# Convolution gate projection by seven products, with weight sums made early and kept in DRAM

## The chip, the cores and the metric

The kernel runs on all 8 cores of one Trainium2 chip (two dies, cores 0 to 3 and 4 to 7). Every core works on its own prompt sequence and its share of the sample rows. A time is the device time of the slowest core in microseconds (us), so one slow core sets it. In this case the granted TensorE clock differs between runs, between chips and between the cores of one run. This text often uses a second measure: the **full-clock span**, the mean span of all cores whose mean granted clock was 0.99 or more, over all timed runs of a kernel on one chip.

## The reference, cut to what matters

A trunk of two layers. The even layer has a pooling mixer and a gated recurrence (HGRN, 6 heads). The odd layer is the gated convolution that is changed here. A squared-ReLU MLP of width 4096 follows each of them: MLP X after the even layer, MLP Y after the odd one.

```python
def odd_layer(h, conv_prev, w_in, conv_w, w_out):       # h: 2048 tokens x 1024 per core
    bg, cg, hv = jnp.split(h @ w_in, 3, axis=-1)         # three 1024 x 1024 projections
    z = cg * hv
    ext = jnp.concatenate([conv_prev, z], axis=1)
    conv = conv_w[0] * ext[:, 0:t_]                      # three taps along the tokens
    for j in range(1, CONV_WIDTH):
        conv = conv + conv_w[j] * ext[:, j:j + t_]
    return (bg * conv) @ w_out, ext[:, -CONV_BUF:]
```

## The kernel before

Most projections go by "seven products" (Strassen's scheme in Winograd's form): a 2x2 block product takes 7 block products instead of 8, for some sums of operands. One group of seven (`quad`) takes 28 matmuls of 128x512 where the straight way takes 32. Its partial results are handed from one PSUM bank to another by a copy on ACT. Ahead of a copy into a bank that its last writer did not fill, the kernel runs one extra identity matmul of 128x512 over that bank (`bits`).

```python
def quad(prods, evac, mark=None, hook=None, raw=False):
    def bits(k):
        if not B_ps[k].full:
            yield MMG([(bank(k), identh, <identity x4>, True, True)], ...)   # 1 matmul 128x512
    def copy(k, src):                                    # "bank copy"
        yield from bits(k)
        op = ACT(bank(k), bank(src), AF.Copy, ...)       # PE must wait for it
    ...
    yield from prod(1, a, True); yield from fifth()
    yield from copy(b, a)
    yield from prod(6, b, False); yield from prod(2, a, False)
    yield from copy(d, b)
    yield from prod(7, d, False)
    ... # cut: products 3, 4 and the evacuations
```

In the convolution only cg and hv went by seven products, one unit per 128 channels; the gate B went straight. DVE made the weight sums inside the stage, and the taps ran on 512 tokens at a time:

```python
def conv_wsums(p):                                       # 4 sums a unit, 16 units
    for c in range(8):
        for o, a, b, op in (("s1","a21","a22",add), ("s2","s1","a11",sub), ("a21","a11","a21",sub), ("s4","a12","s2",sub)):
            yield TT(W[o], W[a], W[b], op, ...)          # 128x512 f16
def conv_bg(p, c, kb):                                   # gate: straight, 16 matmuls a unit
    for t in (2 * p, 2 * p + 1):
        yield MMG([(bank(k), W[bg], hT[:, k8, tokslice(t)], k8 == 0, k8 == 7) for k8 in range(8)], ...)
def taps(D, BD, src, Bsrc, i):                           # in conv_unit, twice a unit
    yield ACT(D, src[:, 0:512], AF.Copy, scale=w0)
    yield STT(D, src[:, 1:513], w1, D, mult, add)
    yield STT(D, src[:, 2:514], w2, D, mult, add)
    yield TT(mixT[:, c, tokslice(t)], bank(kb[i]), D, mult)
```

The order of the instructions on each engine is fixed when the program is built. A list scheduler simulates the engines with modelled durations and a modelled delay from one engine to the next (`HOP`), and emits whichever operation can start first.

```python
HOP = 0.06
start = max(self.free[eng], self.ready(op) + HOP)
# ACT, second part of the program ("late"):
occ = 0.14 + n / 1280.0 + (0.19 if accum is not None else 0.0) + (0.0 if in_psum(in_) else 0.03)
# DVE tensor-tensor:
occ = 0.12 + n / (1925.0 if two else 965.0) + (0.05 if not ps and not two and n > 256 else 0.0)
# a PSUM bank: the one free first; one that still needs bits counts as free 1 us later
return t if want is None or bufs[0].full == want else t + 1.0
```

Of the kernel before, what the change touches and what calls it, by code (L numbers as in the profile page):

```python
# [25 lines left out]
U_OO = 33  # L26
NU = 35
# [7 lines left out]
ROWPAGE = 100  # L35
CPAGES = [0, 5, NPG + 3, NPG + 11]
GPAGES = [10, NPG, NPG + 8]
SHPAGE = NPG + 16
CSP = 11
CSTAGE = 8  # L40
ZSTAGE = 9
# [14 lines left out]
NFIRST = 7  # L56
CLASSIC = 1
M_ORDER = [(0, u) for u in range(U_WO, U_FF0 + 4 * CLASSIC)] + [(1, u) for u in (U_WO, U_WO + 1)]
M_ORDER2 = [(1, u) for u in range(U_CONV, NU)] + [(2, u) for u in range(U_CONV, U_OO)]
# [6 lines left out]
OOPRIO = 299  # L66
FINPRIO = 250
POOLX = 15

HOP = 0.06  # L70
PE_MARGIN = 0.30
# [47 lines left out]
class Prog:  # L119
# [29 lines left out]

    def est(self, op):  # L150
        return max(self.free[op.eng], self.ready(op) + HOP + op.margin)
# [49 lines left out]
    def emit(self, op):  # L201
        eng = op.eng
        start = max(self.free[eng], self.ready(op) + HOP)
        if eng == "pe" and self.filler is not None and start < WARM_END:
            at = max(self.free[eng], max(max(b.wt, b.rt) for b in op.W) + HOP)
            n = int((start - at) * WARM_SHARE / self.filler[0])
            if n > 0:
                make = self.filler[1]
                self.filler = None
                self.emit(make(n, op.W))  # L210
                self.filler = (0.22, make)
                start = max(self.free[eng], self.ready(op) + HOP)
# [182 lines left out]
def build():  # L395
# [15 lines left out]
    w2w = din("w2w", [2, NW2, 4, 128, 2048])  # L411
    gcols_d = din("gcols", [128, 40])
# [27 lines left out]
    with ExitStack() as es:  # L440
# [88 lines left out]
        def ACT(out, in_, func, R, W, scale=1.0, bias=0.0, accum=None, t=None):  # L529
# [5 lines left out]
            if late:  # L535
                occ = 0.14 + n / 1280.0 + (0.19 if accum is not None else 0.0) + (0.0 if in_psum(in_) else 0.03)
                if (not isinstance(scale, float) or not isinstance(bias, float)) and n > 8:
                    occ += 0.09
# [7 lines left out]

        def TT(out, in0, in1, op, R, W, eng="dve", fast=False):
            n = fsz(out)
            if late:
                ps = in_psum(in0) or in_psum(in1)  # L550
                two = not ps and all(a.dtype in (F16, BF16) for a in (in0, in1, out))
                occ = 0.12 + n / (1925.0 if two else 965.0) + (0.05 if not ps and not two and n > 256 else 0.0)
# [7 lines left out]
        def TS(out, in0, s1, op0, R, W, s2=None, op1=None):  # L560
# [4 lines left out]
            occ = 0.134 + fsz(out) / 1800.0 if late else 0.07 + fsz(out) / 1920.0  # L565
            return Op("dve", f, R, W, occ, occ + 0.08)

        def STT(out, in0, scalar, in1, op0, op1, R, W):
            occ = 0.184 + fsz(out) / 964.0 if late else 0.1 + fsz(out) / 850.0
            return Op("dve", lambda e: e.scalar_tensor_tensor(out=out, in0=in0, scalar=scalar, in1=in1,  # L570
                                                              op0=op0, op1=op1), R, W, occ, occ + 0.08)

        def CP(out, in_, R, W, eng="dve"):
            occ = (0.12 if late else 0.07) + fsz(out) / (1925.0 if eng == "dve" else 465.0)
            return Op(eng, lambda e: e.tensor_copy(out=out, in_=in_), R, W, occ, occ + 0.08)
# [82 lines left out]
        for c in range(8):  # L658
            unit_cols[U_CONV + c] = 3072
# [5 lines left out]
        hown = set()  # L665

        def loader(order, pool, mine):
            for key in order:
                it = yield Alloc(pool)
                s = it[0]  # L670
                u = key[1]
                ncol = unit_cols[u]
# [114 lines left out]
        junks = Pool(junk_items[:1])  # L787

        def junk_of(page):

            return pgf(page).bitcast(F16) if page < ROWPAGE else mixT[:, page - ROWPAGE, 0:1024]
# [5 lines left out]
        def norm(b, n, done):  # L797
            jp = junks0 if n == 0 else junks
# [86 lines left out]
        def sample_rows(src, Bs, page, dst, ds):  # L885

            stage = pgf(page, 2)[0:16, :]
            for half in range(2):
# [4 lines left out]
                yield CP(stage[:, half * 512:(half + 1) * 512], bank(k)[0:16, :], [B_ps[k]], pgb(page + half))  # L893
                banks.give(k)
            yield DMA("sp", ds, [(dst, stage)], pgb(page, 2), (), 65536)
# [645 lines left out]

        def quad(prods, evac, mark=None, hook=None, raw=False):
# [67 lines left out]
        def wmlp(tag, l, seq, n_in, n_out, smp, gates):  # L1610
# [14 lines left out]
            if early_t:  # L1625
                cb["h"] = (m02, m12, m03)

            def rings():
                for k in range(NSLOT):
# [9 lines left out]
                    if k == 2:  # L1639
                        cb["h"], cb["w"] = ((m02, m12, m03), (m00, m10, rb[4])) if early_t else ((m00, m10, rb[4]), (m02, m12, m03))  # L1640
# [12 lines left out]
            def w2raw(gi):  # L1653
                return [rb[6], rb[7], rb[8], rb[9]] if gi % 2 == 0 else [ex_blk(1), ex_blk(2), rb[8], rb[9]]
# [17 lines left out]
            def load1():  # L1672
                for n in range(4 * NS):
# [4 lines left out]
                    if n == 3:  # L1678
                        yield up(*gates.get("ex", ()))
# [24 lines left out]
            def combh():  # L1704
                for i, p in enumerate(pairs):
# [15 lines left out]
                    yield up(T("rb", 2))  # L1721
# [39 lines left out]
            def ff1_unit(n):  # L1761
                if True:
# [3 lines left out]
                    if n < 2:  # L1766
                        yield up(T("rb", 0), T("rb", 1), T("rb", 2), *gates["hid"])
# [22 lines left out]
                    def evac(what, k, n=n, gi=gi, u=u, k0=k0, c0=c0):  # L1790
# [12 lines left out]
                        if what in ("12", "22"):  # L1803
                            yield up(T("g", n))
                            yield Op("dve", lambda e: e._custom_dve(TENSOR_ADD_SAT, out=v, in0=bank(k), in1=gst(n), s0=3e38, s1=0.0),  # L1805
                                     [B_ps[k], B_gst[n % 2]], B, 0.68, 0.76)
# [71 lines left out]
            def ff2_quad(m):  # L1878
                if True:
# [8 lines left out]
                    for j in (m % 4,):  # L1888
# [18 lines left out]
                        def evac(what, k, j=j, left=left, last=last, t0=t0, p=p):  # L1907
                            for r, h in {"g": ((0, 1), (1, 1)), "11": ((0, 0),), "12": ((0, 1),), "21": ((1, 0),),
                                         "22": ((1, 1),)}[what]:
# [3 lines left out]
                                left[r] -= 1  # L1913
                                if what == "21" and last and n_out == 4 and p == pairs[-1] and j == 3:
                                    flags.add("lastadd")
                                if left[r] == 0 and last:
                                    if p == pairs[-1]:
                                        S.spawn(norm(b, n_out, ("h%d" % n_out, b)), FINPRIO)
# [89 lines left out]
        def oo():  # L2008
# [15 lines left out]
            t1, t2 = oo_t  # L2024
            t4 = Blk(q4(hg[:, :].bitcast(F16)), [B_hg] * 4)
            yield up("zrows")
            for b in B_oot:
                for pb in flat(pgb(8, 4)):
                    inherit(b, pb)
# [8 lines left out]

            def run(i):
                for p, j in todo[i::2]:  # L2040
                    yield from oo_quad(p, j, b11, b21, b12, b22, t1, t2, t4)
# [3 lines left out]
            for k in keys:  # L2045
                drop(k)

        def oo_sums(p):
# [3 lines left out]
            yield up(*[("cproj", c, t) for c in range(8) for t in (t0, t0 + 1)])  # L2052
# [13 lines left out]
        def oo_norm(b):  # L2066
# [3 lines left out]
            elif b >= 4:  # L2070
                yield up("cquads")
            yield from norm(b, 3, ("h3", b))

        def oo_quad(p, j, b11, b21, t3, b22, t1, t2, t4):
# [3 lines left out]
            yield up("oot", *[("cmix", c, t) for c in range(8) for t in (t0, t0 + 1)])  # L2078
# [10 lines left out]
            def evac(what, k):  # L2089
                for r, h in {"g": ((0, 1), (1, 1)), "11": ((0, 0),), "12": ((0, 1),), "21": ((1, 0),), "22": ((1, 1),)}[what]:  # L2090
# [10 lines left out]
        cva = [[Buf(f"cv{q}{n}") for n in "ABGZ"] for q in range(2)]  # L2101
        B_oot = [Buf("oot0"), Buf("oot1")]

        def conv_s4(p, q):
            if q == 0:
                return band[:, :, :].rearrange("p g t -> p (g t)")[:, 0:512], [B_band]
            if p == 0:
                return hg[:, 0:256].bitcast(F16), flat(B_hg)
            return prevT[:, :, :, :].rearrange("p r c t -> p (r c t)").bitcast(F16), [B_prev]
        oo_t = [Blk(q4(arena[:, 4104 + 1024 * i:5128 + 1024 * i].bitcast(F16)), [[B_oot[i]]] * 4) for i in range(2)]  # L2110

        def conv_bufs(q):
            o = 2052 * q
            A, B, G, Z = arena[:, o:o + 512], arena[:, o + 512:o + 1024], arena[:, o + 1024:o + 1538], arena[:, o + 1538:o + 2052]
            return A, B, G, Z, [[b] for b in cva[q]]

        cwts = {}

        def conv_take(p, c):
            s = slot_of[(1 + p, U_CONV + c)]  # L2120
            W = {}
            for i, n in enumerate(("a11", "a12", "a21", "a22", "bg0", "bg1", "s1", "s2")):
                q = Buf(f"cw{n}")
                src = B_ring[s][i // 4]
                q.w, q.wt = src.w, src.wt
                W[n] = (ring[:, s, 512 * i:512 * i + 512], [q])
            W["s4"] = conv_s4(p, c % 2)
            cwts[p, c] = W

        def conv_put(p, c):  # L2130
            key = (1 + p, U_CONV + c)
            s = slot_of[key]
            for i, n in enumerate(("a11", "a12", "a21", "a22", "bg0", "bg1", "s1", "s2")):
                inherit(B_ring[s][i // 4], cwts[p, c][n][1][0])
            used(key, 2 - p)

        def conv_wsums(p):
            for c in range(8):
                yield loaded((1 + p, U_CONV + c))
                conv_take(p, c)  # L2140
                flags.add(("cw", p, c))
                W = cwts[p, c]
                for i, (o, a, b, op) in enumerate((("s1", "a21", "a22", ALU.add), ("s2", "s1", "a11", ALU.subtract),
                                                   ("a21", "a11", "a21", ALU.subtract), ("s4", "a12", "s2", ALU.subtract))):
                    if o == "s4":
                        if p or c > 1:
                            yield up(("cquad", p, c - 2) if c > 1 else ("cquad", 0, 6 + c))
                        if p:
                            yield up("zrows")
                    yield TT(W[o][0], W[a][0], W[b][0], op, W[a][1] + W[b][1], W[o][1], fast=True)  # L2150
                    flags.add(("cs", p, c, i + 1))

        def conv_t(p):
            return [mix_blk(0, 2), mix_blk(1, 2), mix_blk(0, 3), mix_blk(1, 3)] if p == 0 else \
                [ex_blk(0), ex_blk(1), ex_blk(2), hT_blk(1, 1)]

        def conv_hsums(p):
# [5 lines left out]
            for i, o, a, b, op in ((3, t3, b22, b12, ALU.subtract), (2, t2, t3, b11, ALU.add), (1, t1, b22, t2, ALU.subtract),  # L2163
                                   (4, t4, b21, t2, ALU.subtract)):
                if p and i == 4:
                    yield up(*[("cproj", c, 1) for c in range(8)])
# [3 lines left out]
        def conv_bg(p, c, kb):  # L2170
# [384 lines left out]
```

## Time and profile before

| | before |
|---|---|
| timed runs | 1441.06 us median of 3 (1439.7 to 1441.55) |
| profiled run | span 1415.1 to 1420.7 us by core, granted clock 0.993 to 0.995 |
| busy on core 2 | PE 97%, DVE 80%, ACT 63% |

The page of the kernel before starts with the span and the busy time of each engine; part 4 is the chain of work that ended last.

```profile
span 1420.7 us, 25535 instructions; the slowest of 8 cores (1415.1 to 1420.7 us)
...
PE 1377.5 (97%) x9160; PEld 698.0 (49%) x9182; DVE 1133.3 (80%) x2096; ACT 895.0 (63%) x1806; POOL 189.3 (13%) x274
...
PE 88%; DVE 5%; DMA 2%; ACT 2%; issue 1%; SPq 0%; DVEq 0%; POOL 0%; ACTq 0%; POOLq 0%
...
```

PE is busy 97% of the span and is 88% of the chain. At a given clock only fewer matmuls, or fewer pauses of PE, shorten this kernel. Next, busy time in stretches of the span, still of the kernel before. The first column after the colon is the length, then come PE, PEld, DVE, ACT and POOL busy with the number of instructions, then the granted clock (1.00 is full), the DMA share and GB/s. Rows: MLP X, convolution with the transition to Y, MLP Y.

```profile
...
420.00:775.00 355.00, 351.55 (x2153) 168.07 (x2151) 276.01 (x487) 223.91 (x431) 30.11 (x57) 1.00 0.46 77
775.00:980.00 205.00, 196.48 (x1177) 93.18 (x1176) 182.29 (x386) 98.90 (x187) 15.89 (x30) 0.98 0.45 74
980.00:1400.00 420.00, 419.31 (x2450) 197.35 (x2448) 328.87 (x567) 264.81 (x521) 31.70 (x60) 1.00 0.47 88
...
```

Length minus PE busy is PE's idle time: 3.4, 8.5 and 0.7 us. In the middle row the clock is below full. Next are PE's waits over the whole run (what was waited for: total us, times, longest).

```profile
...
PE pp L598 <- DVE hT L558: 3.8, 2, 2.5
PE pp L598 <- ACT pp L532: 3.3, 5, 1.0
PE pp L600 <- DVE x_sb L558: 2.7, 4, 1.2
...
```

"ACT pp" is a bank copy: PE waits until ACT has moved one PSUM bank into another. The timeline of PE at the transition from the convolution to MLP Y shows where the idle time sits (start, length, group; in brackets the idle time before the group and who ended it).

```profile
...
968.44 1.03 PE L600 MATMUL pp<-arena,hT 128*128 128x512 f16 x4
972.00 0.38 PE L598 MATMUL pp<-identh,arena 128*128 128x128 f16 x4 [2.53 <-DVE hT L558]
973.61 0.59 PE L598 MATMUL pp<-identh,arena 128*128 128x128 f16 x4 [1.22 <-DVE hT L558]
975.40 1.86 PE L600 MATMUL pp<-ring,mixT 128*128 128x512 f16 x4 [1.20 <-DVE x_sb L558]
977.06 1.91 PE L598 MATMUL pp<-arena,hT 128*128 128x512 f16 x4
...
981.18 1.03 PE L598 MATMUL pp<-ring,mixT 128*128 128x512 f16 x4
...
```

PE waits 2.53, 1.22 and 1.20 us for DVE. After that, four matmuls last 1.86 us from first start to last end, where later ones last 1.03: the granted clock was 0.50 from 974 to 979 us (the same view of stretches as above). By start times the next three groups of four take 1.66, 1.70 and 1.13 us instead of 0.86, so 1.9 us are lost to the clock. Before the low clock stood waits of 2.53 and 1.22 us with 0.4 us of small matmuls between them; what sets it off is not shown.

### The profile page before, as it was taken

The numbers are of one execution on the slowest core, as the hardware profiler recorded it, in microseconds if no ns is written. First come the engines' busy times: TensorE is split into PE (matmuls) and PEld (weight loads), VectorE is DVE, ScalarE is ACT, GpSimd is POOL, SyncE is SP. The second block draws the span as 40 slices with busy tenths as digits, with TensorE's granted clock in tenths as the row PEclk, the third lists the DMA queues.
The fourth block names the chain that finished last, engine by engine and source line by source line (L and its number), as shares of the span: only waits on it lengthen the run. The fifth ranks groups of instructions, "written<-read, shape, count | busy, mean of one in ns | idle before, by whom it ended". The sixth has DMA issues, their size and how long they took to land.

```text
span 1420.7 us, 25535 instructions; the slowest of 8 cores (1415.1 to 1420.7 us)
## 1 busy us (share of the span) xinstructions
PE 1377.5 (97%) x9160; PEld 698.0 (49%) x9182; DVE 1133.3 (80%) x2096; ACT 895.0 (63%) x1806; POOL 189.3 (13%) x274
## 2 busy tenths in 40 slices
PE   8989999999999999999999999998999999999996
PEld 3666555654444444454445444444444544444442
DVE  5887898886677778877769999979778788977767
ACT  5868888874455656864667434455647757755655
POOL 1121134333200110010000010000100100100100
PEclk9999999999999999999999999999999999999998
DMA  8681353397644743642633644440735626644612
GB/s 187 158 134 32 89 137 92 93 203 145 153 90 74 120 73 57 109 78 46 116 53 56 101 79 72 67 83 1 126 62 96 105 43 107 163 107 74 119 31 119
DMA packets 64281, 136.68 MB, mean 96 GB/s; under 512 B 6751, under 2 KB 33598, under 8 KB 64142
## 3 DMA queue, kind: packets, MB, share of 16 engines
q0 software_dynamic: 28256, 97.07, 41.0%
q1 hardware_dynamic: 35902, 37.97, 8.7%
q8 instruction: 77, 1.26, 0.4%
q14 instruction: 46, 0.38, 0.1%
HBM read 216.61 MB, written 15.54 MB: 163 GB/s over the span
## 4 chain that ended last, share of the span: by engine, by line
PE 88%; DVE 5%; DMA 2%; ACT 2%; issue 1%; SPq 0%; DVEq 0%; POOL 0%; ACTq 0%; POOLq 0%
PE pp L598 44%; PE pp L600 43%; DMA ring<-wst 1%; PE pp L610 1%; ACT arena L532 1%; DMA x_sb<-xp 1%; DVE hT L558 1%; DVE x_sb L558 1%; DVE arena L558 1%; DVE arena L570 1%; DVE mixT L558 0%; DVE gsm L558 0%; DVE x_sb L570 0%; ACT pp L532 0%; DVE mixT L563 0%
## 5 line engine op out<-in xcount | busy, mean ns | idle before, releaser
L532 ACT ACTIVATE pp<-pp 128x512 f32<-128x512 f32 x432 | 246.4, 581 | 298.8 <-PE pp L598 204.3
L558 DVE TENSOR_TENSOR x_sb<-x_sb,pp 128x512 f32<-128x512 f32 x496 | 322.1, 682 | 92.5 <-PE pp L598 37.0
L600 PE MATMUL pp<-hT,ring 128*128 128x512 f16 (+1 forms) x1700 | 301.0, 318 | 3.8 <-ACT arena L532 1.0
L600 PEld LDWEIGHTS pp<-hT,ring 128*128 128x128 f16 x1700 | 131.6, 97 | 138.0 <-issue 6.2
L532 ACT ACTIVATE arena<-arena 128x512 f16<-128x512 f16 (+1 forms) x287 | 174.2, 623 | 13.2 <-DVE arena L1805 6.6
L532 ACT ACTIVATE arena<-pp 128x512 f16<-128x512 f32 (+3 forms) x224 | 126.9, 574 | 51.5 <-PE pp L600 25.2
L598 PE MATMUL pp<-ring,arena 128*128 128x512 f16 x480 | 120.7, 379 | 0.3
L598 PE MATMUL pp<-hT,ring 128*128 128x512 f16 x456 | 114.8, 379 | 0.6 <-ACT pp L532 0.5
L600 PE MATMUL pp<-ring,mixT 128*128 128x512 f16 x416 | 97.8, 381 | 3.2 <-DVE x_sb L558 1.7
L558 DVE TENSOR_TENSOR hT<-pp,gcols_s 128x512 f16<-128x512 f32 (+1 forms) x96 | 81.9, 862 | 15.7 <-PE pp L598 7.9
L598 PE MATMUL pp<-mixT,arena 128*128 128x512 f16 x368 | 92.9, 379 | 0.2 <-ACT pp L532 0.2
L1805 DVE CUSTOM_DVE_ANT_0 arena<-pp,ring 128x512 f16<-128x512 f32 x106 | 70.1, 683 | 27.8 <-PE pp L598 18.2
L598 PE MATMUL pp<-ring 128*128 128x512 f16 x336 | 85.9, 379 | 0.0
L558 DVE TENSOR_TENSOR arena<-arena 128x1024 f16<-128x1024 f16 (+3 forms) x112 | 70.5, 647 | 14.5 <-ACT arena L532 13.6
L615 POOL DMA_DIRECT2D ring<-w2w x46 | 24.4, 533 | 422.2 <-DVE x_sb L558 139.1
L533 ACT ACTIVATE arena<-x_sb 128x1024 f16<-128x1024 f32 x60 | 63.1, 1052 | 21.1 <-DVE x_sb L558 16.2
L615 POOL DMA_DIRECT2D ring<-wst x73 | 39.7, 550 | 269.8 <-PE pp L600 108.5
L598 PEld LDWEIGHTS pp<-ring,arena 128*128 128x128 f16 x480 | 46.3, 98 | 54.7 <-issue 1.5
L598 PEld LDWEIGHTS pp<-hT,ring 128*128 128x128 f16 x456 | 43.6, 98 | 53.8 <-issue 4.8
L600 PE MATMUL pp<-ring,hT 128*128 128x128 f16 (+2 forms) x960 | 67.5, 227 | 2.1 <-DMA ring<-wst 2.1
L600 PEld LDWEIGHTS pp<-ring,hT 128*128 128x128 f16 (+1 forms) x960 | 60.3, 98 | 8.0 <-issue 3.0
L598 PE MATMUL pp<-mixT 128*128 128x512 f16 x240 | 61.6, 379 | 0.9 <-ACT pp L532 0.9
(258 smaller groups left out, 2303.8 us busy)
## 6 DMA issues: line engine op xcount, KB each, us to landing
ring<-wst POOLq DMA_DIRECT2D x57, 512.0 KB, 7.9
ring<-w2w POOLq DMA_DIRECT2D x46, 512.0 KB, 7.7
ring<-w1w POOLq DMA_DIRECT2D x45, 512.0 KB, 7.5
x_sb<-xp SPq DMA_DIRECT2D x28, 512.0 KB, 6.4
yp<-x_sb SPq DMA_DIRECT2D x16, 512.0 KB, 2.7
extra<-w1w POOLq DMA_DIRECT2D x15, 512.0 KB, 7.4
extra<-w2w POOLq DMA_DIRECT2D x14, 512.0 KB, 10.2
x_sb<-st_hgrn SPq DMA_DIRECT2D x24, 256.0 KB, 4.1
```

The source lines that it names most:

```text
L532: return e.activation(out=out, in_=in_, func=func, bias=bias, scale=scale)
L533: return e.activation(out=out, in_=in_, func=func, bias=bias, scale=scale, accum_out=accum)
L558: return Op(eng, lambda e: e.tensor_tensor(out=out, in0=in0, in1=in1, op=op), R, W, occ, occ + 0.08)
L570: return Op("dve", lambda e: e.scalar_tensor_tensor(out=out, in0=in0, scalar=scalar, in1=in1, op0=op0, op1=op1), R, W, occ, occ + 0.08)
L598: ins = e.matmul(o, l, r, start=s, stop=t, skip_group_check=True)
L600: ins = e.matmul(o, l, r, start=s, stop=t)
L610: ins = e.transpose(out=o, in_=i, identity=idn)
L615: fns = [(lambda e, o=o, i=i: e.dma_start(out=o, in_=i)) for (o, i) in pairs]
L1805: yield Op("dve", lambda e: e._custom_dve(TENSOR_ADD_SAT, out=v, in0=bank(k), in1=gst(n), s0=3e38, s1=0.0), [B_ps[k], B_gst[n % 2]], B, 0. ...
```

## The change

The gate B now also goes by seven products, 28 matmuls for a pair of channel blocks and 1024 tokens, 8 such groups in all. A unit of weights is now a cg/hv unit (8 of them) or a gate pair (4). DVE makes their sums once during MLP X, in the recurrence state's buffer `hg`, from where they go to DRAM (`wsc`); both token halves load ready sums. The conv state is staged in `hg` too, and turned after MLP X's first units. The taps run on 1024 tokens at once. The residual's two adds become one broadcast add. The output projection's weights (OO) are loaded after 7 of the 12 units of the second half. The scheduler gets a new set of durations and hand-over times.

```diff
+CUNITS = [(0, 0), (0, 1), (0, 2), (1, 0), (0, 3), (0, 4), (1, 1), (0, 5), (0, 6), (1, 2), (0, 7), (1, 3)]  # kind 1: gate pair
+OOAT = 7
-M_ORDER2 = [(1, u) for u in range(U_CONV, NU)] + [(2, u) for u in range(U_CONV, U_OO)]
+M_ORDER2 = [... first half ...] + [(2, U_CONV + u) for u in CSEQ[1][:OOAT]] + [(1, U_OO), (1, U_OO + 1)] + [... rest ...]
+HOPS = {"act": 0.034, "dve": 0.034, "pe": 0.145, "pool": 0.08, "sp": 0.08}
+wsc = nc.dram_tensor("wsc", [NCU, 128, 3584], F16, kind="Internal").ap()
 # scheduler, late part
-occ = 0.14 + n / 1280.0 + ...
+occ = n / 1200.0; lat = occ + (0.155 if in_psum(out) else 0.17) ...; occ += (0.052 if ps else 0.093) + ...
-occ = 0.12 + n / (1925.0 if two else 965.0) + ...
+*span(0.066, 0.15, n, two)
+def add_g(b, k):                        # residual: one 128x1024 add, PSUM bank broadcast
+    return TT(x2, x2, bank(k).unsqueeze(1).broadcast_to([128, 2, 512]), ALU.add, ...)
-def conv_wsums(p): ...                  # 64 adds of 128x512 in the stage
+def conv_presum():                      # 96 adds of 128x256 during X
+    for u in range(NCU):
+        for hf in range(2):
+            yield DMA("pool", ..., [(st[:, 0:1024], wst[U_CONV + u, ...])])
+            yield DMA("sp", ..., [(wsc[u, :, o_:o_ + 768], st[:, 0:768])])
+            for o, a, b, op in (...4 sums...): yield TT(V[o], V[a], V[b], op)
+            yield DMA("sp", ..., [(wsc[u, :, o_ + 768:o_ + 1792], st[:, 1024:2048])])
-def conv_bg(p, c, kb): ...
+def conv_bgpair(p, i, u): ...           # quad(conv_prods(p, u), evac)
-yield from taps(B, BB, G, BG, 1) ... yield from taps(A, BA, Z, BZ, 0)
+yield ACT(D, Z[:, 0:1024], AF.Copy, ..., scale=w0)
+yield STT(D, Z[:, 1:1025], w1, D, ...)
+yield STT(D, Z[:, 2:1026], w2, D, ...)
 def conv_state():
-    yield up(*[("pgdone", p) for p in range(NPG)]); stage = pgf(CSTAGE, 4)[0:16, :]
+    yield up("opX", *[("pgdone", p) for p in range(NPG)]); stage = hg[0:32, :]
+    yield DMA("sp", misc(), [(stage, st_conv ...)]); yield up(("X", "u", 1))
 ... # cut: buffers and gates that follow from this
```

## The prediction

> **What bounds the kernel.** TensorE. The page's busy table gives PE 97% of the 1420.7 us span (DVE 80%, ACT 63%); the chain that ended last is 88% PE. In the timeline of PE a group of four 128x512 matmuls takes 0.864 us, 0.216 us each. [...] So only fewer matmuls or less PE idleness shorten the span. PE idles about 43 us (busy by windows): some 26 before 320 us (recurrence), 3.4 between 420 and 775 (MLP X), 8.5 between 775 and 980 (convolution), 0.7 between 980 and 1400 (MLP Y), about 10 at the end. Timed runs take 1441 us, 20 above the profiled one; I take that as common to both.
>
> **What the change does.**
> 1. The convolution's gate projection (B) went straight, 256 matmuls. In pairs by seven products it takes 8 x 28 = 224. 32 x 0.216 = **-6.9 us**, on a saturated PE: critical.
> 2. The convolution's weight sums (64 DVE adds of 128x512 f16, 0.417 us each, 27 us) leave that stage. They are made once in MLP X, as 96 half-size adds (estimate 0.28 us each, from 0.417 and 0.687 us for 128x1024: 27 us), and go through DRAM.
> 3. 64 tap operations of 0.745 us become 32 of about 1.28: -6 us of DVE. Halo copies: -3. The new products add 16 PSUM adds of 0.686: +11. The residual's double add becomes one broadcast operation, two of 0.68 become one of about 1.2, 68 times: -9 over the run. DVE in the convolution stage is 182 of 205 us (89%); I expect about 150. MLP X had 276 of 355 us (78%), becomes about 84%.
> 4. DMA: presums read 12.6 MB and write 11 MB in X, where the DMA share is 0.46; I estimate 0.65. A presum half (load, add, write, one staging buffer) takes an estimated 9 to 11 us; 24 of them, 250 us, fit inside X's 350.
> 5. The output projection now starts among the second half's units, so other matmuls cover the transition to MLP Y. Before, PE waits there about 5 us, mostly for DVE writing the hidden input (waits of PE, 960 to 980 us), and the granted clock falls to 0.83, about 2 us more. I expect about half of this stage's 8.5 + 2 us back: **-4 to -5 us**. New chains (gate pairs wait for taps, three tap buffers) can take some again.
>
> New schedule constants reorder X and Y, but little idleness is left to win there.
>
> **Predicted: 1430 us** (-11), 80% range 1421 to 1439. Faster by over 2%: 0.03; within 2%: 0.95; slower: 0.02.
>
> **What would show it.** 672 instead of 704 wide convolution matmuls; PE busy about 7 us lower; PE idle between X's end and Y's start halved; no DVE adds on ring weights in the convolution; no new PE waits for weights in X.
>
> **What would make it wrong.** [...] Gate pairs hold PSUM banks until the taps are done, which may idle PE in the first half, where no other work fills. If the transition stall and clock dip stay, only 7 us remain; if both vanish, 15 or more.

The sum is -6.9 us (point 1) and -4 to -5 us (point 5), about -11. Point 3's durations have their like in the trace of before: 1.278 us for a 128x1024 operation of the taps' kind on DVE, 1.216 us for a 128x1024 operation of DVE that reads PSUM, 6.5 us in all for DVE's copies of 128x2 (the halos). Point 4's 9 to 11 us are an estimate that the page and trace of before allow: 7.4 us to load 256 KB, 4 x 0.28 us of adds, 2.4 us to write 256 KB.

## The result, and the profile after

| | before | after |
|---|---|---|
| median of the timed runs | 1441.11 us (1439.7 to 1441.55, 4 runs) | 1435.49 us (1435.11 to 1437.02, 4 runs) |
| ratio of fast runs | | 0.9965, 95% interval 0.9947 to 0.9982 |
| full-clock span | 1417.3, 1417.4 and 1417.3 (46 to 92 cores each, later, on three chips) | 1410.8 (10 cores, these runs) |
| 128x512 matmuls in the program | 5505, 12 of them identities | 5481, 20 of them identities |

A ratio is the mean time of one kernel's fast runs over that of the other's of the same rounds, so it is not quite the ratio of the medians. The time lies inside the predicted range. The saving is 5.6 us by medians and 6.5 us at full clock, where 11 were predicted. Spans and clocks of the cores of the kernel after, in the profiled run:

```profile
...
core 1: 1412.8 us, clock 0.996
core 2: 1430.0 us, clock 0.975
...
core 5: 1408.5 us, clock 0.996
...
core 7: 1435.5 us, clock 0.975
...
```

At 0.996 a core takes 1408.5 to 1413 us and at 0.975 about 1430 to 1435.5. So this run's 1435.5 us must not be set against the 1420.7 us of the profiled run of before, whose cores all had 0.993 to 0.995. Later runs of the kernel before show the same gap: its cores at 0.973 to 0.975 took 1435.7 to 1440.0 us. On core 2 of the kernel after the lower clock lies only at the start: 0.85 and 0.84 in the first two stretches of 100 us, 1.00 from 200 to 1380 us. From here on like is compared with like. The page of the kernel after, core 5:

```profile
span 1408.5 us, 25659 instructions; the slowest of 8 cores (1408.5 to 1435.5 us)
...
PE 1368.7 (97%) x9150; PEld 693.9 (49%) x9150; DVE 1127.9 (80%) x2004; ACT 906.4 (64%) x1825; POOL 185.5 (13%) x266
...
PE 83%; DVE 10%; ACT 5%; issue 2%; DMA 0%; SPq 0%; DVEq 0%; ACTq 0%
...
ring<-wsc SPq DMA_DIRECT2D x24, 896.0 KB, 5.4
...
```

The weight sums come back from DRAM in 5.4 us for 896 KB (median of 24 loads, from issue to landing). PE's waits on the same core:

```profile
...
PE pp L625 <- ACT pp L542: 8.9, 17, 1.0
...
PE pp L625 <- DVE mixT L577: 1.8, 1, 1.8
...
```

PE now waits 8.9 us in 17 waits for bank copies, where it waited 3.3 us in 5. The transition to MLP Y in the timeline of PE:

```profile
...
946.35 0.38 PE L625 MATMUL pp<-identh,arena 128*128 128x128 f16 x4 [1.78 <-DVE mixT L577]
946.57 1.89 PE L627 MATMUL pp<-ring,mixT 128*128 128x512 f16 x8
...
951.28 0.38 PE L625 MATMUL pp<-identh,arena 128*128 128x128 f16 x4 [0.65 <-DVE hT L577]
951.50 1.03 PE L625 MATMUL pp<-arena,hT 128*128 128x512 f16 x4
...
```

Two waits of 1.78 and 0.65 us are left, and no matmul runs at half rate any more (granted clock 1.00 from 944 to 956 us): this part did what was hoped. The lost time shows elsewhere. An example in the convolution, from the timeline of all engines:

```profile
...
834.37 2.17 ACT L542 ACTIVATE arena<-arena,convwf_s 128x1024 f32<-128x1024 f32 x2
...
836.45 0.58 ACT L542 ACTIVATE pp<-pp 128x512 f32<-128x512 f32 x1
...
837.17 1.02 PE L625 MATMUL pp<-mixT,ring 128*128 128x512 f16 x4 [1.00 <-ACT pp L542]
...
```

ACT runs two taps of 128x1024 back to back, 2.17 us. The bank copy stands behind them, starts at 836.45, and PE idles 1.00 us.

### The profile page after: what moved, and what is told of

It reads as the page before. It is cut to its first block, busy times and chain, and to the rows that moved or that the text cites. A ratio compares the mean times of both kernels' runs of the same rounds, so it can differ in the third digit from the quotient of the medians.

```text
span 1435.5 us, 25659 instructions; the slowest of 8 cores (1408.5 to 1435.5 us)
## 1 busy us (share of the span) xinstructions
PE 1395.5 (97%) x9150; PEld 705.8 (49%) x9150; DVE 1128.7 (79%) x2004; ACT 909.2 (63%) x1825; POOL 184.9 (13%) x266
## 4 chain that ended last, share of the span: by engine, by line
PE 80%; DVE 10%; ACT 5%; DMA 2%; issue 2%; DVEq 0%; SPq 0%; POOL 0%; POOLq 0%; ACTq 0%
PE pp L627 40%; PE pp L625 38%; ACT arena L542 3%; DMA ring<-w2w 2%; DVE mixT L577 2%; PE pp L637 2%; DVE arena L577 1%; ACT pp L542 1%; DVE x_sb L577 1%; DVE hT L577 1%; DVE arena L595 1%; DVE arena L1847 1%; DVE x_sb L595 1%; DMA gcols_s<-gcols 1%; ACT arena L543 0%
## 5 line engine op out<-in xcount | busy, mean ns | idle before, releaser
L542 ACT ACTIVATE pp<-pp 128x512 f32<-128x512 f32 x456 | 260.2, 583 | 287.2 <-PE pp L625 195.9
L577 DVE TENSOR_TENSOR x_sb<-x_sb,pp 128x512 f32<-128x512 f32 (+1 forms) x392 | 293.2, 775 | 95.2 <-ACT pp L542 43.1
L627 PE MATMUL pp<-hT,ring 128*128 128x512 f16 (+1 forms) x1460 | 266.0, 321 | 1.5 <-ACT arena L542 0.8
L542 ACT ACTIVATE arena<-pp 128x512 f32<-128x512 f32 (+2 forms) x224 | 131.4, 589 | 57.4 <-PE pp L627 35.2
L625 PE MATMUL pp<-hT,ring 128*128 128x512 f16 x648 | 159.9, 379 | 1.3 <-ACT pp L542 1.1
L625 PE MATMUL pp<-mixT,arena 128*128 128x512 f16 x368 | 92.6, 379 | 0.0
L577 DVE TENSOR_TENSOR arena<-arena 128x1024 f16<-128x1024 f16 (+2 forms) x100 | 62.6, 646 | 11.4 <-ACT arena L542 10.6
L625 PE MATMUL pp<-mixT 128*128 128x512 f16 x240 | 61.6, 379 | 5.2 <-ACT pp L542 5.2
L542 ACT ACTIVATE x_sb<-x_sb 128x512 f32<-128x512 f32 (+3 forms) x98 | 54.2, 560 | 13.6 <-DVE x_sb L577 10.2
L627 PE MATMUL pp<-mixT,arena 128*128 128x512 f16 x240 | 61.4, 379 | 0.7 <-DVE arena L577 0.7
L627 PE MATMUL pp<-mixT 128*128 128x512 f16 x240 | 61.6, 379 | 0.0
L625 PE MATMUL pp<-ring 128*128 128x512 f16 x240 | 61.6, 379 | 0.0
```

The lines of the kernel that those rows point to most:

```text
L542: return e.activation(out=out, in_=in_, func=func, bias=bias, scale=scale)
L577: return Op(eng, lambda e: e.tensor_tensor(out=out, in0=in0, in1=in1, op=op), R, W, *span(0.066, 0.15, n, two))
L625: ins = e.matmul(o, l, r, start=s, stop=t, skip_group_check=True)
L627: ins = e.matmul(o, l, r, start=s, stop=t)
```

## The experiments

Eighteen kernels ran, in five calls. The reasons to be tested were these. **C** (constants): the scheduler's new durations and hand-over times put the instructions into an order in which bank copies come later. **W** (wide taps): a tap of 1024 tokens holds ACT for over a microsecond (1.14 us on average in the kernel after, core 5), so a copy behind it comes late. Rivals: the 32 matmuls themselves were worth less than 0.216 us each; the presums' DVE work and traffic cost MLP X; the state's staging did something. The chips differed: the first call ran at a granted clock near 0.93, the second near 0.90 to 0.945, and the other three mostly at 0.995 or 0.975. Where the expectations name a theory by C or W, these are meant. For the first two calls I give spans at a clock of 0.93, from a least-squares line of span against 1/clock over all cores of all runs; their standard errors are 0.2 to 0.5 us. In the second call nearly every run was slow, so its differences are hints.

### a_oldcosts: the change with the old schedule constants

```diff
     def hop(self, eng):
-        return HOPS[eng] if self.late else HOP
+        return HOP
-occ = n / 1200.0 ...                       # ACT, and likewise TT, TS, STT, CP
+occ = 0.14 + n / 1280.0 + ...              # as before the change
```

> The kernel after, with only the schedule's durations for late operations put back to those of before. What is at stake: PE's waits for bank copies on ACT, 3.3 us in 5 waits before and 8.9 us in 17 waits after on an undisturbed core. Theory W (wide taps: a tap operation of 1.1 us on ACT stands in front of the copies) expects those waits to stay at 8 to 10 us and the time within 1.5 us of the kernel after. Theory C (the new constants made the order worse) expects the waits to fall to 3 to 4 us and the time to fall by about 5 us. A third outcome, slower by 2 to 5 us, would say that the constants paid for themselves.

Measured: 1498.34 us against 1509.9 of before, ratio 0.9926 [0.9902, 0.9949]. At clock 0.93: 1490.6 against 1499.1, so 8.5 us less. PE's waits for bank copies were 2.4 us in 4 waits. This kernel beats the one before.

### a_halftaps: the change with taps of 512 tokens

```diff
-yield ACT(D, Z[:, 0:1024], AF.Copy, ..., scale=w0)
-yield STT(D, Z[:, 1:1025], w1, D, ...)     # and the third tap
+for q in (0, 512): yield ACT(D[:, q:q + 512], Z[:, q:q + 512], AF.Copy, ..., scale=w0)
+for o, wt in ((1, w1), (2, w2)):
+    for q in (0, 512): yield STT(D[:, q:q + 512], Z[:, q + o:q + o + 512], wt, D[:, q:q + 512], ...)
```

> The kernel after, with each 1024-wide tap operation (one on ACT, two on DVE) issued as two 512-wide ones: the same work and 48 more fixed costs, no longer than 0.75 us each. Theory W expects 2 to 4 us less PE idleness between 770 and 980 us, and the time 2 to 3 us below the kernel after. Theory C and the theory that gate pairs hold PSUM banks (theory B) expect no gain: within 1 us, or slower because DVE has about 6 us more to do there.

Of the fixed costs the traces show this: two taps of 512 take 2 x 0.745 us on DVE and 2 x 0.716 on ACT (before, core 2), one of 1024 takes 1.279 and 1.139 (after, core 5).

Measured: 1502.21 us, ratio 0.9946 [0.9919, 0.9974]; at clock 0.93 1492.0, bank-copy waits 5.9 us in 8. With no run of the kernel after beside it, W stayed undecided.

### a_more32: eight times four matmuls more

In each of the 8 gate groups the first product of four matmuls is done twice, which leaves the result as it was.

```diff
+if twice and i == 1:
+    yield MMG([(bank(k), l, r, j == 0, j == n - 1) for j, (l, r) in enumerate(mm)], R, [B_ps[k]])
```

> The kernel after, with the first product of each gate pair computed twice into its bank: 32 matmuls of 128x512 more (30 by the static count, since two fewer identity matmuls come with it), no more data, no more copies. If PE bounds that stage, 30 x 0.216 = 6.5 us slower (5 to 8). If the stage is bound by the chain of copies and taps, the matmuls fall into the waits and it is less than 3 us slower; then the saving of 32 matmuls was worth as little.

Measured: 1509.67 us, nearly all runs slow (one of 1663.04 us with a die at a clock of 0.82), no ratio. Inconclusive, and repeated (a_more32b).

### b_newcosts: the kernel before with the new constants

The reverse of a_oldcosts's edit, made in the kernel before.

> The kernel before, with only the new schedule durations for late operations. Its static count of identity matmuls rises from 12 to 24, 12 x 0.216 = 2.6 us of PE. Theory C expects it 3 to 6 us slower than before, with PE's waits for bank copies rising from 3.3 us towards 8. Theory W expects those waits unchanged at 3 to 4 us and about 2 us slower, or faster if the order is better otherwise.

Measured: 1518.39 us, ratio 1.0039 [1.0011, 1.0067]: slower. PE's waits:

```profile
...
PE pp L631 <- DMA arena<-st_conv: 9.5, 1, 9.5
PE pp L619 <- ACT pp L536: 8.4, 11, 2.7
...
```

The 9.5 us are one wait for the load of the conv state into the pages: the new order asks for it too early. This fits with the change moving the state's staging. The bank copies went from 3.3 to 8.4 us without any wide tap. So the constants make such waits by themselves. What these waits cost is another matter: at clock 0.93 this kernel is 11.3 us slower than before, and the one long wait and 12 more identity matmuls (2.6 us by count) make up 12.1.

### a_again: the kernel after once more

> The kernel after itself, unchanged: the runs so far fell on a chip that grants about 0.93 of the clock instead of 0.98 to 0.99, and the kernel after has no time there. Expected about 0.994 to 0.996 of the kernel before. Theory C expects it clearly above the variant with the old constants (0.9926 of before on that chip), at 0.995 or more; theory W expects no difference from that variant.

Measured: 1538.54 us, all runs slow, before 1550.0; at clock 0.93 1490.6 against 1499.9, 9.3 us less. This is as good as a_oldcosts's 8.5 on the other chip. At this clock theory C found no support.

### a_both: old constants and halved taps together

The edits of a_oldcosts and a_halftaps in one kernel.

> Old schedule constants and half-width taps together, in the kernel after. If the two remove different waits, about 3 us below the variant with the old constants alone (0.990 to 0.991 of before). If the constants alone made the waits (theory C), no gain from the taps: 0.992 to 0.994. PE's waits for bank copies 2 to 4 us in both cases.

Measured: 1552.51 us; at clock 0.93 1499.9, no better than before (1499.9), which neither expectation allowed for. The two edits do not add up; by this line, nothing is left of the change's gain. New waits stood in the trace: 3.5 us for DVE writing `extra` (the sums of the second token half) and 1.7 us for ACT's norm, at the border of the two token halves.

### b_newcosts_state: before, new constants, and the new staging of the state

```diff
-stage = pgf(CSTAGE, 4)[0:16, :]
+stage = hg[0:32, :]
+yield up(("X", "u", 1))
-hid=("opX", "prev", *pgs)
+hid=("opX", *pgs)
```

> The kernel before with the new schedule constants and with the new handling of the convolution state (staged in the recurrence state's buffer, turned behind X's first units). The same constants without the new state handling made PE wait 9.5 us for the DMA of the state. If that wait was all of their cost, this one is equal to before within 2 us, plus 10 more identity matmuls, 2.3 us: 1.000 to 1.002. If the constants cost by themselves (theory C), 1.003 or more. The wait for the state's DMA should be gone in either case.

Measured: 1541.67 us, slow; at clock 0.93 1501.1, 1.2 us above before (1499.9). The 9.5 us wait is gone and the bank copies still take 7.4 us in 10 waits. By its own expectation this speaks against C in the kernel before: ten more identity matmuls alone are 2.2 us by count, so the longer waits for bank copies cost nothing that shows at this clock. The staging takes away a wait that only the new constants made; no other gain shows.

### a_onesum: only one unit's sums are made

All units load unit 0's sums, so the result is wrong (relative error 1.4), but 11 of 12 parts of the presums are gone.

```diff
-for u in range(NCU):
+for u in range(1):
-    (ring[:, s, 0:3584], wsc[u - U_CONV])
+    (ring[:, s, 0:3584], wsc[0])
```

> The kernel after with the weight sums made for the first convolution unit only; all units load that one's (wrong result on purpose in y and the convolution outputs). It takes away 11 of 12 presums: 88 of 96 adds on DVE, about 11.5 MB of reads and 10 MB of writes in X. If presums cost X something (weights late behind presum loads on the POOL queue), 2 to 5 us faster than the kernel after; by my prediction they are off the path: within 1.5 us.

Measured: 1543.76 us; at clock 0.93 1494.9, 4.3 us slower than a_again with less work, which the expectation did not allow for. PE's idle time in MLP X (core 2, 420 to 800 us) fell from 1.7 in a_again to 0.6 us, so on this core, at a clock of 0.90, the presums cost about 1 us there. On core 3 PE waits 4.8 us for DVE writing `extra` and 3.5 us for ACT's norm, waits of the kind that a_both had.

### b_again1, a_again3, a_oldcosts3, a_keepbanks1: four kernels on one chip, mostly undisturbed

The first two are the kernels before and after unchanged, the third repeats a_oldcosts. The fourth makes the scheduler avoid identity matmuls:

```diff
-return t if want is None or bufs[0].full == want else t + 1.0
+return t if want is None or bufs[0].full == want else t + 2.0
```

> The kernel before, unchanged, for its trace on the same chip as the next three. Expected equal to before (ratio 1.000). On a chip that grants less clock PE is slower and ACT is not, so PE's waits for bank copies should be at most the 3.3 us of the first trace, and the wait at the change from convolution to MLP Y about the same 5 us.

> The kernel after, unchanged, beside the kernel before and its old-constants variant. Expected 0.993 to 0.996 of before. At equal granted clock (span against clock over all cores) 6 to 9 us below before. PE's waits for bank copies 5 to 9 us[...]; wait before MLP Y about 2.5 us.

> The kernel after with the old schedule constants, repeated on the same chip as the kernel after. Theory C in its strong form (the new constants cost the missing 5 us) expects 3 to 5 us below the kernel after at equal clock. Since the first run showed 2.4 us of bank-copy waits but 5 us of waits for DVE instead, I now expect a difference below 2 us either way: the constants move the waits rather than make them.

> The kernel after with one number of the bank choice changed: a bank that was last written in part (it then needs an identity matmul of 128x512 before a chain of copies may use it) is only taken when it is 2 us earlier, not 1 us. Static count: 10 identity matmuls instead of 20, so 10 x 0.216 = 2.2 us of PE less. If the extra identity matmuls are the missing part of the saving on PE, 1.5 to 3 us below the kernel after; if the later banks cost waits instead, no gain or slower.

| kernel | median us | ratio to before [95%] | full-clock span | 128x512 matmuls | bank-copy waits (core 1) |
|---|---|---|---|---|---|
| b_again1 | 1433.9 (fast runs 1420.7 to 1422.7) | 1.0004 [0.9986, 1.0022] | 1417.1 | 5505 | 3.7 us / 6 |
| a_again3 | 1415.0 | 0.9957 [0.9943, 0.997] | 1410.7 | 5481 | 9.0 us / 17 |
| a_oldcosts3 | 1412.45 | 0.9937 [0.9925, 0.9949] | 1407.6 | 5478 | 3.0 us / 7 |
| a_keepbanks1 | 1414.14 | 0.9948 [0.9935, 0.9962] | 1409.5 | 5471 | 8.5 us / 16 |

Six runs of three of the kernels were slow (1445 to 1665 us); the ratios leave them out. The chip gave its full clock (0.992 to 0.998 by core in the four profiled runs), which b_again1's expectation had not foreseen. What that expectation says of PE and ACT is so on two cores of the kernel after: a bank copy takes 582 ns on average on core 5 at 0.996 and 583 on core 7 at 0.975, while PE is busy 1368.7 and 1395.5 us.

At full clock the old constants are worth 3.1 us (1410.7 against 1407.6), of which 0.6 are three matmuls; I had expected less than 2. Ten identity matmuls less, 2.2 us by count, gave 1.2, less than the 1.5 to 3 expected. Stretches of core 1, first of b_again1, then of a_again3, then of a_oldcosts3 (convolution, then transition to Y):

```profile
...
770.00:930.00 160.00, 155.25 (x980) 74.38 (x981) 142.00 (x309) 73.66 (x139) 16.45 (x32) 1.00 0.51 83
930.00:1000.00 70.00, 64.90 (x331) 30.30 (x330) 63.05 (x113) 39.43 (x74) 2.64 (x5) 0.95 0.19 32
...
```

```profile
...
770.00:930.00 160.00, 155.28 (x986) 74.55 (x985) 133.88 (x219) 93.52 (x171) 3.81 (x8) 1.00 0.50 152
930.00:1000.00 70.00, 67.37 (x383) 32.12 (x382) 62.74 (x103) 43.94 (x83) 4.62 (x9) 1.00 0.34 59
...
```

```profile
...
770.00:930.00 160.00, 156.54 (x990) 74.99 (x989) 134.82 (x218) 93.65 (x169) 4.74 (x9) 1.00 0.53 154
930.00:1000.00 70.00, 67.55 (x401) 32.35 (x399) 63.70 (x105) 44.76 (x89) 3.69 (x7) 1.00 0.24 44
...
```

In the transition PE idles 5.1, 2.6 and 2.4 us, and the clock is 0.95, 1.00 and 1.00. In the convolution it idles 4.7, 4.7 and 3.5 us (of the kernel before, core 1 idles most here; its cores idle 3.2 to 4.8 us, so the mean in the table below is lower). PE's waits of a_oldcosts3 on this core:

```profile
...
PE pp L619 <- ACT pp L542: 3.0, 7, 0.8
PE pp L621 <- DVE arena L578: 2.8, 4, 1.3
...
```

The waits for bank copies are down to 3.0 us. Some came back as waits for DVE (arena: 2.8 us; before 2.2), so 6 us of waits taken away gave half of that. The account of PE's idle time by stretch, mean of all 8 cores (length less busy time, summed from the same view for every core):

| stretch | before (b_again1) | after (a_again3) | old constants (a_oldcosts3) |
|---|---|---|---|
| 0 to 400, recurrence | 14.6 | 16.0 | 14.35 |
| 400 to 770, MLP X | 5.0 | 5.4 | 5.55 |
| 770 to 930, convolution | 3.85 | 4.8 | 3.7 |
| 930 to 1000, transition | 5.2 | 2.55 | 2.45 |
| 1000 to 1380, MLP Y | 0.5 | 1.8 | 1.4 |
| 1380 to the end | 11.3 | 11.7 | 11.0 |
| all idle | 40.5 | 42.2 | 38.5 |
| PE busy | 1376.6 | 1368.8 | 1368.7 |
| span | 1417.1 | 1411.0 | 1407.2 |

PE works 7.8 us less after the change and idles 1.7 us more. The transition gave 2.65 us; every other stretch took, 4.4 us in all. With the old constants the others take only 0.75 us.

### a_halftaps2, a_more32b, a_ooat0, a_old_keepbanks: the open parts at full clock

The first two repeat edits told above. a_ooat0 sets OOAT from 7 to 0, so the output projection's weights come ahead of the second half's units as before the change. a_old_keepbanks joins a_oldcosts and a penalty of 4.0 in the choice of banks.

> The kernel after with half-width taps. On the first chip its bank-copy waits were 5.9 us in 8 waits at a granted clock of 0.93. On a chip at 0.99 theory W expects PE's bank-copy waits between 770 and 930 us to fall from the kernel after's 3 us to below 1.5 us and the time 1.5 to 3 us below the kernel after (0.9957 of before on such a chip), so 0.993 to 0.995. If the constants make these waits, they stay and the ratio is 0.995 to 0.998.

> The kernel after with 32 matmuls of 128x512 more in the gate pairs (30 net of identity matmuls). At full clock 30 x 0.216 = 6.5 us above the kernel after, so 1.000 of before (0.998 to 1.002), if each matmul costs its full time there.

> The kernel after with the output projection's weights loaded ahead of the second half's convolution units, as before, instead of after seven of them. My prediction said that the later start lets other matmuls cover the change to MLP Y. If so, PE's waits between 930 and 1000 us rise from 2.6 us to about 5 us and the granted clock dips there as before: 2 to 4 us above the kernel after. If the order of loads does not matter, within 1 us.

> The best candidate: the kernel after with the old schedule constants and with the penalty for partly written banks at 4 us, which leaves 13 identity matmuls where the old constants alone leave 17. Expected 0.9 us below the old constants' variant from PE's work alone: 0.993 of before (0.991 to 0.995) on a chip at 0.99.

Before, on this chip: median 1439.73 us (1420.25 to 1468.73), full-clock span 1417.4. Its runs mixed two clocks, so the ratios are too wide to use (0.9961 [0.988, 1.0042], 0.9956 [0.9897, 1.0015], 1.0043 [0.9947, 1.014], 1.0029 [0.9892, 1.0166]) and I compare full-clock spans, with 1410.7 for the kernel after.

**a_halftaps2**: 1413.0 us, 2.3 more. PE's waits in the convolution:

```profile
...
PE pp L627 <- DVE hT L577: 1.8, 1, 1.8
PE pp L625 <- ACT pp L542: 1.7, 2, 1.6
PE pp L625 <- ACT arena L542: 1.1, 1, 1.1
PE pp L627 <- DVE arena L577: 0.8, 1, 0.8
...
```

In a_again3 this stretch had 3.3 us in 6 waits for bank copies; now it is 1.7 in 2. So W is right about single waits. But 1.8 us for DVE writing hT, 1.1 and 0.8 us came in their place: PE's idle time in the convolution rose from 4.8 to 6.3 us (mean of 8 cores). Taking W's waits away won nothing, so W gets no support as the cause of the loss.

**a_more32b**: 1415.9 us, 5.2 more for 30 matmuls (32 more, two identities fewer), 6.5 by count. Idle time in the convolution fell from 4.7 to 3.0 us. So 30 matmuls on this PE cost about 80% of their price; the edit also redraws the order, so the share is rough. The rival that matmuls are worth little falls.

**a_ooat0**: 1413.2 us, 2.4 more. But not for the reason that I had: the waits at the transition did not come back.

```profile
...
PE pp L627 <- DVE x_sb L577: 0.7, 2, 0.5
...
PE pp L625 <- ACT pp L542: 0.6, 1, 0.6
```

PE idles 1.9 us from 930 to 1000, and the clock stays at 1.00. In the convolution it idles 5.9 us instead of 4.7 and in Y (1000 to 1380) 2.4 instead of 1.6 (core 1). So the later load of the output projection's weights did not shorten the transition. DVE's relief and the new gates of Y's first norms remain as candidates; no run separates them.

**a_old_keepbanks**: wrong result (relative error 0.33 in the prompt's conv state, 0.06 in y_prompt). Its time (1444.5 us) says nothing.

### a_oldhop and a_olddur: each half of the constants alone

```diff
 # a_oldhop: hand-over times as before, new durations
-        return HOPS[eng] if self.late else HOP
+        return HOP
 # a_olddur: old durations (as in a_oldcosts), but
+        return HOPS[eng] if self.late else HOP
```

> The kernel after with only the scheduler's new hand-over times put back to the one old value of 0.06 us; the new durations of the instructions stay. It splits the 3.1 us that all old constants together gave (mean span of the cores at a clock of 0.99 or more: 1410.7 with the new ones, 1407.6 with the old). Theory C1 (the hand-over times are what costs: PE's copies of a bank are placed too late behind other work of ACT): 1407 to 1408.5, PE's waits for the bank copies of ACT near 3 us of 9. Theory C2 (the shorter durations of ACT are what costs): 1410 to 1411.5, these waits stay at 8 us or more. Rival R (no constant is at fault by itself; each set of constants draws another order of the same work, and orders differ by some 3 us): anything from 1407 to 1414, and the two runs of this call do not add up to 3.1.

> The complement: the old durations of the instructions, the new hand-over times. Theory C1: 1410 to 1411.5 at a clock of 0.99 or more, waits for bank copies 8 us or more. Theory C2: 1407 to 1408.5 and these waits near 3 us. Rival R: anything from 1407 to 1414; both runs at the same side of 1409.1, or one outside 1407 to 1411.5, speaks for R.

Before, on this chip: full-clock span 1417.3. a_olddur: 1427.04 us median, ratio 1.0003 [0.9878, 1.0129], full-clock span 1420.7, which is 10 us above the kernel after; bank-copy waits 10.0 us in 16. a_oldhop: 1476.94 us (one fast run, 1454.14), full-clock span 1449.1, 38 us above, and a wrong result (0.46 in the prompt's conv state). Neither half brings the 3.1 us; each alone is much worse than both or none. The times fit neither C1 nor C2 (a_olddur's waits are as C1 said, its time is not). R's mark, a run outside 1407 to 1411.5, is there; but both runs also lie far outside R's own range of 1407 to 1414, so orders differ by much more than the 3 us that R allowed. As a_oldhop is wrong, this rests on a_olddur alone. No single constant is shown to be at fault. Two stretches of a_oldhop:

```profile
...
440.00:520.00 80.00, 79.91 (x357) 32.66 (x355) 59.27 (x105) 38.78 (x72) 8.45 (x16) 1.00 0.58 107
870.00:880.00 10.00, 2.28 (x20) 1.62 (x18) 8.18 (x12) 5.41 (x11) 0.00 (x0) 0.64 0.19 77
880.00:890.00 10.00, 9.07 (x29) 3.42 (x30) 3.65 (x5) 2.85 (x5) 0.00 (x0) 0.68 0.00 0
...
```

At the border of the token halves PE idles 7.7 of 10 us (4.8 us for DVE `extra`, 3.4 for ACT's norm, the waits that a_both and a_onesum had), and the clock falls to 0.64 and 0.68. And in MLP X, at a clock of 1.00 and almost without idle time, PE finishes 357 matmuls in 80 us, where the kernels before and after finish 372. In the timeline some groups of four start 1.02 us apart instead of 0.86. Such pauses count as busy. They make an estimated 25 of the 30 us by which PE's busy time grew: 15 matmuls of 0.216 us in 80 us of MLP X, and 15 in 120 us of MLP Y (540 against 555 in b_again1, 1240 to 1360 us), taken over the 370 and 380 us of the two. What makes these pauses is not shown. As the result is wrong, this run shows only how far an order can go.

## Why the prediction was right or wrong

**What bounds the kernel: right.** 30 added matmuls cost 5.2 us at full clock. The 0.216 us of a matmul are those of the trace of before: groups of four 128x512 start 0.86 us apart.

**Point 1, "32 x 0.216 = -6.9 us": the term was too large.** The projection lost 32 matmuls, but the new order wants 20 identity matmuls where 12 were enough. The count of the program is 24 lower: -5.2 us. I had counted the groups in the diff, not what `bits` adds.

**Points 2 to 4: costs of single instructions right, DVE's load by stage wrong.** The sums of 128x256 took 0.282 us (estimate 0.28), the broadcast add 1.215 (about 1.2), a wide tap on DVE 1.279 (about 1.28). MLP X's DMA share rose (on core 1, 400 to 770 us, from 0.48 to 0.67; estimate 0.65), and no new wait for weights appeared there. But DVE was forecast at about 150 of the 205 us from 775 to 980 us and at 84% of MLP X, 298 us. In the same stretches of core 5 it is busy 180.0 us (before, core 2: 182.3) and 277.8 us (276.0). Other work came into the freed time: 12 of the 96 sums still ran after 775 us, and 30 writes of hT stood in the convolution's stretch where 20 had.

**Point 5, "about half of this stage's 8.5 + 2 us back: -4 to -5 us": near in size, for a reason that fell.** The transition's idle time shrank by 2.65 us and the clock dip of 1.9 us went: 4.6 us. The convolution, which belongs to the stage of the forecast, idled 0.95 us more, so the stage won 3.6. The reason was that the output projection "now starts among the second half's units". It already did so in the kernel before. The timeline of DVE shows there the first add of the output projection's result and the start of the convolution's last tap:

```profile
...
903.93 0.67 DVE L558 TENSOR_TENSOR x_sb<-x_sb,pp 128x512 f32<-128x512 f32 x1
...
965.24 0.74 DVE L570 SCALAR_TENSOR_TENSOR arena<-arena,convwf_s 128x512 f32<-128x512 f32 x1
...
```

In the kernel after (core 5) the same two are:

```profile
...
915.18 1.21 DVE L577 TENSOR_TENSOR x_sb<-x_sb,pp 128x1024 f32<-128x1024 f32 x1
...
941.16 1.27 DVE L595 SCALAR_TENSOR_TENSOR arena<-arena,convwf_s 128x1024 f32<-128x1024 f32 x1
...
```

The output projection starts 11 us later, not earlier, while the last tap starts 24 us earlier. In a_ooat0 (925.9 and 939.5 us, core 0) and a_oldcosts3 (928.2 and 937.1, core 1) the transition is as short. So what these three share is the earlier end of the taps; that it shortened the transition is not shown, as no run moved it alone.

**The step that failed: "New schedule constants reorder X and Y, but little idleness is left to win there."** I asked only what a new order could win and booked zero. It could also lose, and the other stretches took 4.4 us: recurrence 1.4, X 0.4, convolution 0.95, Y 1.3, end 0.4. With the old constants the same change gives 9.7 us at full clock (1417.3 to 1407.6), close to the forecast of 11. The identities of point 1 (1.7 us) and the constants (3.1, of which 0.6 are three of the same identities) make 4.2 of the 4.5 us missing at full clock.

Where the order loses is less clear. PE's waits for bank copies grew from 3.7 to 9.0 us on core 1 (MLP X 1.7 to 4.4, convolution 1.8 to 3.3, Y 0.2 to 1.1), and in the example above the copy stands behind two taps on ACT. But X's idle time grew by only 0.4 us, so there these waits mostly took the place of others, and in the recurrence and at the end, with 1.8 of the 4.4 us, PE waits for no bank copy. The recurrence's 1.4 us is the least certain part: the cores of a_again3 alone idle 14.3 to 18.6 us there. And a_keepbanks1 had 8.5 us of such waits and beat the kernel after. That the bank copies are the loss is not shown.

The sum at full clock, means of 8 cores: -5.2 (24 matmuls) -1.9 (clock dip) -0.7 (other PE work, not separated) -2.65 (idle at the transition) +4.4 (idle elsewhere) = -6.05; measured 1417.1 to 1411.0, -6.1.

**What stays open.** The new constants as a set cost 3.1 us at full clock. It is not shown that one of them is at fault: undoing either half alone made it worse by 10 and 38 us, and at a clock of 0.93, on two different chips, no difference showed (8.5 and 9.3 us saved). The fair reading is that nearly the same work has many orders, which differ by more than the whole gain. Correct ones at full clock ran 1407.6, 1409.5, 1410.7, 1413.0, 1413.2 and 1420.7 us. What shortened the transition, and why two orders give wrong results, is open too; the latter deserves to be found before any reordering of this kernel is trusted.

The best version was a_oldcosts: the change with the old constants, correct, ratio 0.9937 [0.9925, 0.9949] to the kernel before. It beat both kernels at full clock.

## What to carry to other kernels

When a change also alters the scheduler's model, price the new order as a risk in every stage, not only as a chance where idle time is left: removing or moving one wait here (halved taps, earlier weights, fewer sums) mostly made another. Count instructions in the built program, as extra ones (the identities) can eat a quarter of a saving. And before comparing spans, compare clocks: 0.996 against 0.975 was 20 us here, three times the effect.
